# A hybrid decoder step on one core: another port rule in the planner, other feed-forward groups, squares summed by matmul, another attention order

## The chip, the cores and the metric

One core of a Trainium2 chip runs the whole program. The metric is the device time in microseconds of one execution. Of the kernel before there are three runs, and their median is the number that the change is measured against.

## What is computed

The reference is one inference step of a two-layer decoder trunk in fp32, for a prompt of 512 tokens and 8 samples of 8 new tokens each, at a width of 1024.

```python
def rms_norm(x, g):
    y = xf * lax.rsqrt(jnp.mean(xf * xf, axis=-1, keepdims=True) + EPS)
...
def swiglu(h, w_in, w_out):
    gate, up = jnp.split(h @ w_in, 2, axis=-1)
    return (jax.nn.silu(gate) * up) @ w_out
...
    for l in range(DEPTH):
        sh1, sc1, g1, sh2, sc2, g2 = ada_mod(c, ada_w[l], ada_b[l], 6)
        h = modulate(rms_norm(x, norm_g[l, 0]), sh1, sc1)
        if l < N_A_LAYERS:
            out, nbuf, h_last = recurrent_block(h, ...)
        else:
            q = apply_partial_rope((h @ attn_w_q[j]).reshape(B, T, N_HEADS, HEAD_DIM), pos)
            out = sliding_sink_attention(q, k_all, v_all, attn_sinks[j], p0) @ attn_w_o[j]
        x = x + g1[:, None, :] * out
        h = modulate(rms_norm(x, norm_g[l, 1]), sh2, sc2)
        x = x + g2[:, None, :] * swiglu(h, ffn_w_in[l], ffn_w_out[l])
```

After layer 0 a projection of the normalised stream gives keys and values, which layer 1 attends to over a window of 128. The feed-forward width is 2816, which is 22 chunks of 128.

## The kernel before, in words

The tokens are cut into two halves, h = 0 and h = 1 (A and B in the attention order), each of 256 prompt tokens and 32 sample tokens, 288 columns. The stream x lies transposed: 8 chunks of 128 features by 288 tokens for each half. Every large product is made of a rounded high part and a rest of each operand (`split`), and takes three matmuls for each chunk of 128 rows. So weights are first cast on ScalarE (ACT) into a high part and subtracted on VectorE (DVE) into a low part (`convert`, `operand`), and PE runs some 8000 matmuls of 288 columns.

The stages follow each other: start and adaLN products; the recurrent block in the order of the string `RNN` (x: conv inputs, g: the gates of a chunk, y: the gelu branch); its output product with residual; feed-forward layer 0; keys and values; queries and attention in the order of the string `ATT`; attention's output product; feed-forward layer 1; the last norm.

No engine call is issued where it stands. `Engine.record` (from L385) stores each with an estimated cost, and all appear in the profile under its line, L442. `Recorder.schedule` (from L213) then plans all of them as a list scheduler: at each step it takes for each engine, among the ready operations (up to 24 looked at), one with an early start and a low number, and emits the operations in the order of the planned starts. The plan knows the buffers, the delays between engines, and a port that DVE and GpSimd (POOL) share: an operation with `op.port` set starts no earlier than 130 ns before the port's last holder ends (L300) and then holds it (L331). `port` is set at L400 for POOL operations that read SBUF and for DVE operations with two wide SBUF inputs; an input that is also the output isn't counted. A changed cost or rule therefore moves instructions on all engines, in the whole program.

The places that the change touches besides:
- `square` (L778) squares a chunk of x on ACT after its residual and adds it on DVE to acc; `stats` (L789) sums over the features with three fp32 matmuls of acc with a vector of ones (one column out, for 128, 128 and 32 tokens), and `spread` takes the power on POOL, transposes it over the partitions on PE and copies it by ACT. `stats` is called for both halves after the recurrent block's output, after feed-forward 0 (`after_ffn0`, for keys and values) and after attention's output: six calls.
- `gates` (L1065) casts a chunk of the conv output into ta (ACT), subtracts into tb (POOL), and PE multiplies both with the gate weights; activations and a scan on DVE follow. Before it `evac_xr` does the conv: three SCALAR_TENSOR_TENSOR steps on DVE, in place, and small copies of carried columns on POOL.
- `ffn` (L1164) makes 22 chunks of the inner layer, and after each group of them (`GROUPS`, 6, 6, 6 and 4 chunks) the eight output units of that group for both halves (`out`): a unit is 3 matmuls for each chunk of the group, then a residual step. In the last group half 0 runs ahead by `LEAD` = 4 units.

## Time and profile before

| | us |
|---|---|
| median of 3 runs | 1288.2 (1283.86 to 1288.42) |
| the profiled execution: its time | 1286.79 |
| its span | 1285.0 |
| PE busy | 1247.7 (97%) |
| DVE busy | 891.7 (69%) |
| ACT busy | 655.9 (51%) |
| POOL busy | 485.7 (38%) |

The profiled execution's own time is 1.8 us above its span (what lies around the span) and 1.4 us under the median. Its mean granted TensorE clock is 0.987 of full speed. Of the chain of work that ended last, PE is 80% of the span, DVE 8% and ACT 5%. A busy share is a mean over stages, so the windows and timelines of the rows further below matter more than it.

### The profile page before, as it was taken

To read this page: it belongs to the slowest core of one execution; us is meant where nothing else is said; L and a number is where in the kernel's file an instruction comes from. 1 tells how busy PE (TensorE), PEld (TensorE's weight loads), DVE (VectorE), ACT (ScalarE), POOL (GpSimd) and SP (SyncE) were. 2 spreads that over 40 slices of the span, in tenths; PEclk is the share of its full clock that TensorE was granted. 3 is DMA by queue.
4 is the path that set the end of the run, shared out by engine and by line. 5 is a ranking of instruction groups with operands and counts; after the bars stand their busy time and mean duration, and the time that the engine had idled before them with its cause. 6 is when DMAs were issued, how large, how long until landed. Compare 5 with 4: busy or idle time off the path is not lost.

```text
span 1285.0 us, 25432 instructions
## 1 busy us (share of the span) xinstructions
PE 1247.7 (97%) x9532; PEld 1176.5 (92%) x9532; DVE 891.7 (69%) x2161; ACT 655.9 (51%) x1468; POOL 485.7 (38%) x710
## 2 busy tenths in 40 slices
PE   7898999999999999999999999999999999999997
PEld 5697889999999999999999988799999999999997
DVE  6886886687557546745769878657965765775767
ACT  4776884575234424522548668637642542552433
POOL 3455551114245135414424535200334633642422
PEclk9998999999999999999999999999999999999998
DMA  9944536335545755554441330323142332233222
GB/s 306 333 149 148 188 109 212 113 106 163 182 132 143 221 162 180 160 169 158 123 115 35 71 92 14 105 83 124 55 130 63 99 115 73 77 108 91 72 94 74
DMA packets 223981, 165.40 MB, mean 129 GB/s; under 512 B 23757, under 2 KB 209065, under 8 KB 223826
## 3 DMA queue, kind: packets, MB, share of 16 engines
q1 hardware_dynamic: 223410, 163.45, 42.1%
q8 instruction: 75, 1.23, 0.4%
q0 software_dynamic: 448, 0.32, 0.1%
q14 instruction: 48, 0.39, 0.1%
HBM read 160.85 MB, written 4.87 MB: 129 GB/s over the span
## 4 chain that ended last, share of the span: by engine, by line
PE 80%; DVE 8%; ACT 5%; POOL 2%; DMA 2%; issue 2%; SPq 1%; ACTq 0%; DVEq 0%; POOLq 0%
PE mm L442 76%; PE ada L442 4%; DVE sl L442 2%; DVE wh L442 2%; DVE ta L442 1%; POOL sl L442 1%; DMA raw<-in_ffn_w_in_dram 1%; DVE tb L442 1%; ACT tb L442 1%; ACT sl L442 1%; ACT wh L442 1%; ACT h L442 1%; SPq L442 1%; DMA reg<-in_x_prompt_dram 1%; ACT L442 1%
## 5 line engine op out<-in xcount | busy, mean ns | idle before, releaser
L442 PE MATMUL mm<-h,wh 128*128 128x288 f32 x4128 | 598.7, 300 | 9.7 <-DVE wh L442 5.6
L442 PEld LDWEIGHTS mm<-h,wh 128*128 128x128 f32 x4128 | 566.0, 190 | 27.8 <-issue 11.3
L442 PE MATMUL mm<-sl,wh 128*128 128x288 f32 x3218 | 459.5, 296 | 0.9 <-DVE sl L442 0.9
L442 PEld LDWEIGHTS mm<-sl,wh 128*128 128x128 f32 x3218 | 436.3, 188 | 7.5 <-issue 5.9
L442 ACT CAST wh<-raw 128x512 fp32r<-128x512 f32 (+2 forms) x388 | 268.0, 710 | 308.3 <-PE mm L442 210.2
L442 DVE TENSOR_TENSOR wh<-raw,wh 128x512 fp32r<-128x512 f32 (+2 forms) x388 | 346.4, 914 | 54.7 <-ACT wh L442 50.1
L442 DVE SCALAR_TENSOR_TENSOR x<-mm,mods,x 128x256 f32<-128x256 f32 x160 | 77.2, 482 | 149.9 <-PE mm L442 149.7
L442 POOL TENSOR_TENSOR raw<-raw 128x512 f32<-128x512 f32 x76 | 110.0, 1449 | 183.8 <-DVE wh L442 183.2
L442 POOL TENSOR_TENSOR x<-x,ta 128x32 f32<-128x32 f32 x152 | 53.5, 352 | 305.6 <-DVE ta L442 305.5
L442 POOL TENSOR_TENSOR raw<-raw,raw 128x512 f32<-128x512 f32 x76 | 112.3, 1477 | 3.8
L442 PE MATMUL mm<-tb,wh 128*128 128x288 f32 (+1 forms) x488 | 89.9, 299 | 5.9 <-POOL tb L442 5.0
L442 PEld LDWEIGHTS mm<-tb,wh 128*128 128x128 f32 x488 | 73.4, 190 | 7.7 <-POOL tb L442 5.5
L442 POOL TENSOR_TENSOR td<-td,td 128x288 f32<-128x288 f32 x38 | 31.9, 840 | 109.0 <-ACT td L442 109.0
L442 PE MATMUL mm<-ta,wh 128*128 128x288 f32 (+1 forms) x254 | 57.2, 302 | 0.0
L442 ACT ACTIVATE ta<-x 128x288 f32<-128x288 f32 x56 | 24.7, 444 | 56.4 <-POOL x L442 53.3
L442 DVE TENSOR_TENSOR td<-mm,td 128x288 f32<-128x288 f32 x76 | 33.8, 454 | 28.0 <-PE mm L442 27.8
L442 PE MATMUL ada<-reg,cz 128*32 128x512 f32 (+1 forms) x448 | 50.3, 553 | 0.2
L442 PEld LDWEIGHTS mm<-ta,wh 128*128 128x128 f32 x254 | 42.5, 191 | 3.4 <-ACT ta L442 1.7
L442 ACT COPY td<-mm 128x256 f32<-128x256 f32 (+1 forms) x102 | 33.2, 351 | 21.7 <-PE mm L442 18.7
L442 ACT ACTIVATE ta<-ta,stat 128x256 f32<-128x256 f32 (+2 forms) x72 | 32.3, 470 | 21.4 <-DVE stat L442 21.1
L442 DVE TENSOR_TENSOR sl<-td,sl 128x288 fp32r<-128x288 f32 x50 | 39.1, 782 | 6.0 <-ACT sl L442 5.4
L442 DVE TENSOR_TENSOR ta<-ta,mm 128x288 f32<-128x288 f32 x38 | 17.2, 453 | 28.8 <-PE mm L442 28.8
(202 smaller groups left out, 1249.1 us busy)
## 6 DMA issues: line engine op xcount, KB each, us to landing
raw<-in_ffn_w_in_dram SPq DMA_DIRECT2D x88, 512.0 KB
reg<-in_ada_w_dram SPq DMA_DIRECT2D x80, 512.0 KB
raw<-in_ffn_w_out_dram SPq DMA_DIRECT2D x48, 384.0 KB
raw<-in_rnn_w_in_dram SPq DMA_DIRECT2D x16, 512.0 KB
reg<-in_kv_ada_w_dram SPq DMA_DIRECT2D x16, 512.0 KB
wh<-in_ada_w_dram SPq DMA_DIRECT2D x24, 256.0 KB
raw<-in_rnn_w_out_dram SPq DMA_DIRECT2D x8, 512.0 KB
raw<-in_ffn_w_out_dram SPq DMA_DIRECT2D x16, 256.0 KB
```

The costliest lines, as they stand in the source:

```text
L442: self.rec.add(eng, lambda: getattr(obj, name)(*map(real, args), **{k: real(v) for k, v in kw.items()}), cost, outs, ins, func, lat, port, ...
```

## The change

Four parts. (1) In the planner, an operation's `port` is 0, 1 or 2. In-place inputs count now, so the conv steps on DVE are port operations. A DVE operation may start 130 ns before the port comes free, a POOL operation only 20 ns after it. POOL operations of up to 40 elements (`port` 2) don't hold the port; if it is held, their planned cost grows by the wait. (2) The square of the last chunk stays in a buffer of its own (`sq7`) instead of being added to acc, and `stats` has three more matmuls with ones for it. (3) The feed-forward groups are 5, 5, 6 and 6 chunks. (4) Another order of the jobs in attention.

```diff
--- before.py
+++ after.py
@@ -50,8 +50,8 @@
 WIN = 600
 
 RNN = "x0 x1 x2 g0 g1 x3 y0 y1 x4 g2 g3 x5 y2 x6 y3 g4 g5 x7 y4 y5 g6 g7 y7 y6"
-ATT = ("q0A q1A a0A q0B q2A a1A q1B a0B q3A a2A q2B a1B q4A a3A q3B a2B q5A a4A q4B a3B q6A a5A q5B a4B q7A a6A s0A q6B a5B s1A "
-       "a7A s2A q7B s3A s0B a6B fA s1B o0A s2B a7B s3B o1A fB o2A")
+ATT = ("q0A q2A a0A q1A q0B a2A a1A q1B q3A a0B q2B a1B q4A a3A a4A q3B a2B q5A q4B a3B q6A a5A q5B q7A a6A a4B s0A "
+       "q6B a5B s1A s2A s3A q7B a7A s0B a6B fA s2B a7B s1B o0A s3B o1A fB o2A")
 LOOK = {"PE": 24, "DVE": 24, "ACT": 24, "POOL": 24, "SP": 24}
 NRAW = 4
 NSL, NTA, NTB, NTD = 37, 7, 8, 4
@@ -230,6 +230,7 @@
         nxt = {k: 0 for k in self.kinds}
         got = set()
         cold = 0.0
+
 
         port, mode = 0.0, 0
         pos = {n: j for k in self.order for j, n in enumerate(self.order[k])}
@@ -297,8 +298,8 @@
                             break
                         continue
                     s = max(f, op.ready, at)
-                    if op.port:
-                        s = max(s, port - 130)
+                    if op.port == 1:
+                        s = max(s, port - 130 if e == "DVE" else port + 20)
                     if e == "PE" and op.mode != mode:
                         s = max(s, f + 100)
                     sw = e == "ACT" and op.func and op.func not in FREE_FUNCS and (table[0] is None or op.func not in TABLES[table[0]][1])
@@ -328,8 +329,10 @@
                 got.add(n)
             op.start = s
             cost = op.cost
-            if op.port:
+            if op.port == 1:
                 port = s + cost
+            elif op.port == 2 and s + 60 < port:
+                cost += port - s
             if e == "PE":
                 mode = op.mode
             if e == "PE":
@@ -396,8 +399,10 @@
         ps_ = any(_is_psum(x) for x in ins)
         func, lat = None, 0
 
-        wide = [x for x in ins if not _is_psum(x) and not str(x.space).endswith("DRAM") and (_free(x) > 1 or f == 1)]
+        reads = [x for x in (list(args) if "out" in kw else list(args[1:])) + [v for n, v in kw.items() if n not in ("out", "accum_out")] if isap(x)]
+        wide = [x for x in reads if not _is_psum(x) and not str(x.space).endswith("DRAM") and (_free(x) > 1 or f == 1)]
         port = eng == "POOL" and name != "dma_start" and bool(wide) or eng == "DVE" and not ps_ and (len(wide) > 1 or name == "tensor_scalar" and f > 1)
+        port = (2 if eng == "POOL" and f <= 40 else 1) if port else 0
         mode = 0
         if name == "matmul":
             if kw.get("start") is not True:
@@ -774,22 +779,30 @@
         return t.rearrange("p (b t) -> p b t", b=4)
 
 
+    sq7 = [None, None]
+
     def square(h, c):
         if c == 0:
             S.activation(acc[h][:], x[h][:, c, :], AF.Square)
         else:
             s = ta()
             S.activation(s.f[:, 0:HC], x[h][:, c, :], AF.Square)
-            V.tensor_tensor(acc[h][:], acc[h][:], s.f[:, 0:HC], ALU.add)
-            s.done()
+            if c == KC - 1:
+                sq7[h] = s
+            else:
+                V.tensor_tensor(acc[h][:], acc[h][:], s.f[:, 0:HC], ALU.add)
+                s.done()
 
     TOK = [slice(0, P), slice(P, 2 * P), slice(2 * P, HC)]
 
     def stats(h):
+        st = tst[h][:, 0:3]
         pt = aux()
-        st = tst[h][:, 0:3]
-        for t, ts in enumerate(TOK):
-            T.matmul(pt[0 : ts.stop - ts.start, t : t + 1], acc[h][:, ts], ones, start=True, stop=True)
+
+        for i, y in enumerate((acc[h], sq7[h].f)):
+            for t, ts in enumerate(TOK):
+                T.matmul(pt[0 : ts.stop - ts.start, t : t + 1], y[:, ts], ones, start=i + t == 0, stop=i == 1, skip_group_check=True)
+        sq7[h].done()
         V.tensor_scalar(st[:, 0:2], pt[:, 0:2], 1.0 / D, EPS, ALU.mult, ALU.add)
         V.tensor_scalar(st[0:32, 2:3], pt[0:32, 2:3], 1.0 / D, EPS, ALU.mult, ALU.add)
         spread(h)
@@ -1159,7 +1172,7 @@
 
 
 
-    GROUPS, PLAIN = (6, 6, 6, 4), 3
+    GROUPS, PLAIN = (5, 5, 6, 6), 3
 
     def ffn(l, g, after):
         wi, wo = a["ffn_w_in"][l], a["ffn_w_out"][l]
```

What this moves, at three places (the helper that records every operation is L442 before and L447 after). First the recurrent block's first gates, on PE. mm29 and mm30 are the two gate products of chunk 0, mm31 and mm32 those of chunk 1; ta is the cast and tb the rest of the conv output; mm34 and mm35 are other large products. Before:

```order
L442 MATMUL mm29_942<-ta29_926,wh19_718 128x300
L442 MATMUL mm29_942<-ta29_926,wh20_836 128x300
L442 MATMUL mm30_947<-ta29_926,wh21_771 128x300
L442 MATMUL mm30_947<-ta29_926,wh22_864 128x300
L442 MATMUL mm29_942<-tb25_934,wh19_718 128x300
L442 MATMUL mm30_947<-tb25_934,wh21_771 128x300
L442 MATMUL mm31_958<-ta31_932,wh19_718 128x300
L442 MATMUL mm31_958<-ta31_932,wh20_836 128x300
L442 MATMUL mm32_965<-ta31_932,wh21_771 128x300
L442 MATMUL mm32_965<-ta31_932,wh22_864 128x300
```

Now the first rows, and the rows around the tb products:

```order
L447 MATMUL mm29_931<-ta29_914,wh19_719 128x300
L447 MATMUL mm29_931<-ta29_914,wh20_819 128x300
L447 MATMUL mm30_939<-ta29_914,wh21_775 128x300
L447 MATMUL mm30_939<-ta29_914,wh22_857 128x300
L447 MATMUL mm34_944<-h01_323,wh23_918 128x288 x2
L447 MATMUL mm31_952<-ta31_937,wh19_719 128x300
L447 MATMUL mm31_952<-ta31_937,wh20_819 128x300
...
L447 MATMUL mm35_843<-h11_441,wh14_616 128x288
L447 MATMUL mm35_843<-h11_441,wh13_603 128x288 x2
L447 MATMUL mm29_931<-tb25_1020,wh19_719 128x300
L447 MATMUL mm30_939<-tb25_1020,wh21_775 128x300
L447 MATMUL mm35_843<-h11_441,wh14_616 128x288
```

The tb products stood right behind the ta products; now 39 large products of mm34 and mm35 and the ta products of chunk 1 stand between (the rows left out are of the same kinds). On POOL, 18 small operations of the conv stand between the last subtraction of h and the one into tb25, 13 before; on DVE the low part wh24 stands behind ten of the conv's steps, before behind twelve.

Second, DVE at the weight whose low part is wh36 (mm56 in the row of the high part wh35 on PE). ta and sl are gate operands of chunks, td11 a conv input. Before:

```order
L442 SCALAR_TENSOR_TENSOR sl25_1234<-sl26_1469,hA_81,ta38_1220 128x300
L442 TENSOR_TENSOR ta43_1403<-ta43_1403,sl34_1482 128x300
L442 SCALAR_TENSOR_TENSOR sl31_1352<-sl32_1479,ta41_1347 128x300
L442 TENSOR_TENSOR ta44_1452<-ta44_1452,sl25_1234 128x256
L442 SCALAR_TENSOR_TENSOR sl33_1415<-sl34_1482,ta43_1403 128x300
L442 TENSOR_TENSOR ta44_1452<-ta44_1452,sl25_1234 128x32
L442 SCALAR_TENSOR_TENSOR sl38_1574<-td11_1165,vecT_74,sl38_1574 128x300 x2
L442 TENSOR_TENSOR sl36_1643<-ta44_1452,sl35_1627 128x288
L442 SCALAR_TENSOR_TENSOR sl38_1574<-td11_1165,vecT_74,sl38_1574 128x300
L442 TENSOR_TENSOR wh36_1650<-raw18_1112,wh35_1559 128x1024
```

Now:

```order
L447 SCALAR_TENSOR_TENSOR sl37_1493<-td10_1110,vecT_74,sl37_1493 128x300
L447 SCALAR_TENSOR_TENSOR sl17_1031<-tb36_1517,sl17_1031 128x300
L447 SCALAR_TENSOR_TENSOR sl37_1493<-td10_1110,vecT_74,sl37_1493 128x300 x2
L447 TENSOR_TENSOR wh36_1556<-raw18_1127,wh35_1539 128x1024
L447 SCALAR_TENSOR_TENSOR tb36_1517<-sl33_1522,sl34_1530 128x300
L447 SCALAR_TENSOR_TENSOR sl38_1558<-td11_1158,vecT_74,sl38_1558 128x300
L447 SCALAR_TENSOR_TENSOR ta38_1260<-ta38_1260,sl16_965 128x300
L447 SCALAR_TENSOR_TENSOR ta41_1328<-ta41_1328,sl10_898 128x300
L447 TENSOR_TENSOR ta38_1260<-ta38_1260,sl26_1397 128x300
L447 TENSOR_TENSOR ta41_1328<-ta41_1328,sl32_1405 128x300
```

The steps of ta38, ta41 and ta43 with their SCALAR_TENSOR_TENSOR rows (scans among them) stood ahead of wh36; now they come behind it.

Third, PE at the end of feed-forward 0, from half 0's sums of squares (mm249) to the first key/value product (h03); mm250 holds the transposes of `spread`, mm251 to mm255 are the last output units. Before:

```order
L442 MATMUL mm253_8317<-sl201_8045,wh269_8174 128x288
L442 MATMUL mm249_8342<-small_67,acc0_69 128x1 x2
L442 MATMUL mm249_8342<-small_67,acc0_69 32x1
L442 MATMUL mm254_8350<-sl189_7633,wh270_8191 128x288
L442 MATMUL mm254_8350<-sl190_7649,wh270_8191 128x288
...
L442 MATMUL mm254_8350<-sl202_8053,wh270_8191 128x288
L442 MATMUL mm250_8370<-ident_66,tst0_71 128x128 x2
L442 MATMUL mm250_8370<-ident_66,tst0_71 128x32
L442 MATMUL mm254_8350<-sl201_8045,wh271_8200 128x288
...
L442 MATMUL mm255_8379<-sl202_8053,wh272_8252 128x288
L442 MATMUL mm255_8379<-sl201_8045,wh273_8265 128x288
L442 MATMUL mm258_8436<-h03_8412,wh274_8282 128x288
L442 MATMUL mm259_8438<-h03_8412,wh278_8346 128x288
```

Now:

```order
L447 MATMUL mm248_8234<-sl203_7954,wh273_8232 128x288
L447 MATMUL mm249_8264<-small_67,acc0_69 128x1 x2
L447 MATMUL mm249_8264<-small_67,acc0_69 32x1
L447 MATMUL mm251_8212<-sl198_7861,wh264_7898 128x288
...
L447 MATMUL mm252_8279<-sl185_7384,wh266_7930 128x288
L447 MATMUL mm249_8264<-small_67,ta245_8277 128x1 x2
L447 MATMUL mm249_8264<-small_67,ta245_8277 32x1
L447 MATMUL mm252_8279<-sl186_7405,wh266_7930 128x288
...
L447 MATMUL mm253_8317<-sl181_7249,wh269_8119 128x288
L447 MATMUL mm250_8323<-ident_66,tst0_71 128x128 x2
L447 MATMUL mm250_8323<-ident_66,tst0_71 128x32
L447 MATMUL mm253_8317<-sl185_7384,wh268_8106 128x288
```

Before, 11 large products stood between the sums and the transposes, and 13 between the transposes and the first product of h03. Now 9 stand between acc's sums and those of the last square (ta245), 17 from there to the transposes, and 51 from the transposes to the first product of h03.

## Rows read from the trace of the kernel before

**Rows 1.** The page, busy us, share of the span and instructions of each engine.

```profile
PE 1247.7 (97%) x9532; PEld 1176.5 (92%) x9532; DVE 891.7 (69%) x2161; ACT 655.9 (51%) x1468; POOL 485.7 (38%) x710
```

**Rows 2.** Windows: span, busy us (instructions) per engine, granted clock, DMA share, GB/s.

```profile
660.00:680.00 20.00, 16.54 (x113) 15.53 (x112) 15.44 (x44) 13.17 (x28) 7.48 (x14) 0.95 0.46 116
680.00:700.00 20.00, 20.00 (x149) 19.74 (x149) 17.53 (x49) 14.75 (x40) 7.59 (x9) 0.97 0.19 41
780.00:800.00 20.00, 19.41 (x174) 16.86 (x174) 15.03 (x65) 17.75 (x65) 12.57 (x25) 1.00 0.08 22
800.00:820.00 20.00, 17.81 (x134) 13.72 (x130) 13.48 (x63) 13.98 (x54) 8.40 (x24) 0.91 0.36 103
1000.00:1020.00 20.00, 20.00 (x152) 20.00 (x152) 15.61 (x24) 11.41 (x25) 13.65 (x10) 1.00 0.32 90
```

**Rows 3.** The same table for the recurrent block, and the sum over it.

```profile
60.00:80.00 20.00, 19.17 (x127) 17.97 (x127) 12.84 (x22) 14.35 (x29) 11.08 (x26) 0.83 0.50 157
...
100.00:120.00 20.00, 15.97 (x112) 13.01 (x105) 14.76 (x27) 12.34 (x26) 14.23 (x32) 0.87 0.67 217
120.00:140.00 20.00, 19.90 (x147) 18.22 (x146) 14.57 (x31) 15.17 (x28) 9.42 (x22) 0.96 0.31 97
...
160.00:180.00 20.00, 18.01 (x134) 16.16 (x133) 15.98 (x27) 15.74 (x30) 11.93 (x25) 0.99 0.25 79
180.00:200.00 20.00, 19.84 (x140) 19.61 (x139) 18.43 (x40) 15.92 (x26) 8.29 (x23) 0.93 0.74 227
sum 140.00, PE 131.39 PEld 120.40 DVE 109.96 ACT 105.79 POOL 75.41; mean PE 18.77 PEld 17.20 DVE 15.71 ACT 15.11 POOL 10.77
```

**Rows 4.** Timeline of PE, 52 to 62: start, length, instruction, [idle time before, releaser].

```profile
60.83 0.87 PE L442 MATMUL mm<-tb,wh 128*128 128x300 f32 x2 [2.99 <-POOL tb L442]
```

**Rows 5.** Timeline of DVE, 52 to 62.

```profile
53.58 5.38 DVE L442 SCALAR_TENSOR_TENSOR sl<-td,vecT,sl 128x300 f32<-128x300 f32 x12
```

**Rows 6.** Timeline of POOL, 52 to 62.

```profile
54.10 0.49 POOL L442 COPY xtail<-td 128x3 f32<-128x3 f32 x1
...
58.54 3.01 POOL L442 TENSOR_TENSOR tb<-sl,ta 128x300 fp32r<-128x300 f32 x2
61.50 0.18 POOL L442 COPY pco<-td 128x3 f32<-128x3 f32 x1
```

**Rows 7.** Timeline of PE, 108 to 118.

```profile
116.54 1.81 PE L442 MATMUL mm<-h,wh 128*128 128x288 f32 x6 [4.03 <-DVE wh L442]
```

**Rows 8.** Timeline of DVE, 108 to 118.

```profile
115.28 1.21 DVE L442 TENSOR_TENSOR wh<-raw,wh 128x1024 fp32r<-128x1024 f32 x1
```

**Rows 9.** Timeline of POOL, 108 to 118.

```profile
112.93 2.10 POOL L442 TENSOR_TENSOR tb<-sl,ta 128x300 fp32r<-128x300 f32 x2
```

**Rows 10.** Timeline of PE, 170 to 180.

```profile
179.36 0.52 PE L442 MATMUL mm<-tb,wh 128*128 128x300 f32 x1 [1.99 <-POOL tb L442]
```

**Rows 11.** Timeline of POOL, 170 to 180.

```profile
175.64 1.85 POOL L442 COPY ho<-sl 128x1 f32<-128x1 f32 x4
```

**Rows 12.** Timeline of PE, 664 to 682.

```profile
668.89 0.73 PE L442 MATMUL mm<-small,acc 128*128 128x1 f32 x6
669.54 1.71 PE L442 MATMUL mm<-sl,wh 128*128 128x288 f32 x11
671.90 0.60 PE L442 MATMUL mm<-ident,tst 128*128 128x128 f32 x3 [0.65 <-POOL tst L442]
...
677.19 4.98 PE L442 MATMUL mm<-h,wh 128*128 128x288 f32 x24 [2.77 <-ACT h L442]
```

**Rows 13.** Timeline of POOL, 664 to 682.

```profile
669.95 1.90 POOL L442 TENSOR_TENSOR tst<-tst,small 128x3 f32<-128x3 f32 x1 [1.52 <-DVE tst L442]
```

**Rows 14.** Timeline of PE, 1270 to 1286.

```profile
1275.33 1.01 PE L442 MATMUL mm<-ident,x 128*128 128x128 f32 x6 [0.54 <-DVE ta L442]
1276.70 0.76 PE L442 MATMUL mm<-small,acc 128*128 128x1 f32 x6 [0.36 <-DVE acc L442]
```

**Rows 15.** Timeline of PE, 798 to 818.

```profile
806.19 0.32 PE L442 MATMUL mm<-ta,reg 128*64 128x160 f32 x1 [2.12 <-ACT sl L442]
```

## The prediction

> **What bounds the kernel now.** I read the busy row of the page first. TensorE (PE) is busy 97% of the span, VectorE (DVE) 69% [rows 1]. So time can come from three places: instructions that PE no longer executes, stretches in which PE stands idle, and stretches in which it runs at the lower of its two clock levels (1.2 instead of 2.4 GHz). Then I read the table of 20 us windows. Its first number after the length is PE's busy time, and the granted clock stands before the DMA share. In the feed-forward part a window is full (20.00 us, 152 rows, so a product every 0.132 us) at clock 1.00 [rows 2]: nothing is to be had there. The lost time lies in the recurrent block (60 to 200 us) [rows 3], at the hand-over to the key/value part (660 to 700) and at the end of attention (800 to 820) [rows 2], each with idle time and a clock under 1. Last I read the timelines of PE at these places, where the bracket gives the idle time and its releaser, and the timelines of the engine named.
>
> Four stalls carry the argument.
> - S1: PE idles 2.99 us before the product with the gate remainder tb, which comes from POOL [rows 4]. POOL was late because its small copies took 0.49 us each while DVE ran twelve three-operand conv steps back to back [rows 5, 6]; the same copy takes 0.18 us when DVE is at something else [rows 6].
> - S2: PE idles 4.03 us for a weight's low part from DVE [rows 7]. That subtraction takes 1.21 us and began only at 115.28 [rows 8], behind steps of DVE that alternated with two POOL subtractions (2.10 us for two) [rows 9].
> - S3: 1.99 us, again for tb from POOL [rows 10], which stood behind four copies that took 1.85 us [rows 11].
> - S4: after the sums of squares PE idles 0.65 us for POOL's power and then 2.77 us for the first normalised chunk [rows 12]; the power itself takes 1.90 us [rows 13].
>
> The lower clock adds to this. A window of 20 us at clock c loses 20(1-c): 3.4 us in 60:80; 2.6 + 0.8 in 100:120 and 120:140; 0.2 + 1.4 in 160:180 and 180:200 [rows 3]; 1.0 + 0.6 in 660:680 and 680:700; 1.8 in 800:820 [rows 2]. Of the first two a part (0.4 and 1.0 us by my estimate) fell into the idle time itself. So S1 is worth 6.0 us, S2 6.4, S3 3.6, S4 5.0; S1 to S3 together 16.0.
>
> **The change, part by part.** All times stand against the profiled execution, 1286.8 us; the median of the runs is 1288.2, 1.4 us above, and I move the sum over unchanged.
>
> *Scheduler's port rule, S1.* PE's last product before the wait ended at 60.83 - 2.99 = 57.84 [rows 4]. Now 39 other products and the four of the next chunk's first half stand between the gate's first half and its tb products, so PE comes to them at 57.84 + 43 x 0.132 = 63.5. POOL has five more small instructions ahead of tb: its start moves from 58.54 to 61.1 at most (5 x 0.52), and with 1.5 us for one of the two [rows 6] tb is there by 62.6. The inserted products need weight wh24, whose low part moved up on DVE from behind the twelfth conv step to behind the tenth: ten steps of 0.45 us from 53.6 [rows 5] and 1.2 us for the part end near 59.3, and PE, with 16 products from 57.3 on, arrives there near 59.4. I take all of S1: -6.0 (bounds 0, if the wait reappears at the next tb, and -6.0).
>
> *S2.* The weight's low part (wh36) now stands ahead of the chain of steps it was behind, and products stand ahead of the adaLN group. But everything that was ahead of it is still to be done by the same two engines: busy time in 60:200 is 110 us on DVE and 75 on POOL of 140 (the sum in [rows 3]). I take half: -3.2 (bounds 0 and -6.4).
>
> *S3 and what the gates get in exchange.* Its tb comes 60 products earlier than its use, but three other tb's in the middle of the stage are now issued late and their products deferred. S3 going (-3.6) against a new wait of the size of S3: 0 (bounds -3.6 and +3.6). For the deferred gates, whose scans end 26 products (26 x 0.132 = 3.4 us) later at the end of the stage, I add +1.5 (bounds 0 and +3.4). Recurrent block: -6.0 - 3.2 + 0 + 1.5 = -7.7.
>
> *Groups of 5, 5, 6, 6: S4.* The number of products does not change; the number of output units and evacuations does not either, and their loads carry the same bytes in other pieces (of 64 KB for each chunk of a unit). What changes is that a unit of the last group has 18 products instead of 12, so that the lead of four units is 72 products instead of 48. In the new order the chain from the last sum to the transposes has 17 products beside it (2.2 us; it took 669.54 to 671.90, 2.36 us [rows 12]), and the one from there to the first key/value product has 51 (6.7 us, against 677.19 - 671.90 = 5.3 us). Both idle times and the lower clock after them go: -5.0 (bounds -3 if the transposes still wait, and -5.0). The second half's sums come with products behind them; no stall. Inside the two feed-forward layers: 0, since PE is full there [rows 2]; bounds -1 and +2 for loads that come later or earlier.
>
> *The tail.* At the end DVE falls behind units of 12 products (1.6 us each); PE idles 0.54 and 0.36 us for it [rows 14]. With 18 products (2.4 us) DVE keeps up: -0.9 (bounds 0 and -0.9).
>
> *Squares.* Six calls of the sums get three more products with ones each; DVE loses six adds, of which none is named as a releaser of PE in the rows. Three such products moved the next one from 668.89 to 669.54, 0.65 us [rows 12]. PE is full where they stand, so they cost 6 x 0.65 = +3.9 (bounds 0, if they only fill idle time, and +4.4). The Trainium skill ("TensorE: Matmul & The Clock Gate", section "Back-to-back issue gap") gives a product of 1 to 64 columns some 60 cycles, 25 ns; two instructions for each product make 0.15 us a call and +0.9 us in all, and by that the sum below would be 3.0 us lower. The row contradicts it here, so the row counts. The new products wait for ACT's square of the last chunk; they are queued 9 products behind the first three at S4, so nothing waits behind them there.
>
> *Attention's order.* Before, the run of small transposes and score products with no large product beside it is, counted in the order of PE's instructions, 87 long at the end, and PE idles 2.12 us in it [rows 15] and loses 1.8 us by the clock [rows 2]. Now the longest runs are 70 at the end and 42 earlier. A run of 34 lies in 780:800, where PE lost 0.6 us [rows 2]. The end may gain up to 4, the new run may lose as much: 0 (bounds -4 and +4).
>
> **Sum:** -7.7 - 5.0 - 0.9 + 3.9 + 0 + 0 = -9.7, so 1277.1 for the profiled execution and **1278.5 us** for the median.
>
> **The rivals.** (a) *The shared port is full.* POOL's copies and DVE's two-input steps slow each other [rows 6, 9], so in the recurrent block an order cannot help if together they need the whole stage; the stalls only move. Their busy times, 185 us in 140, speak for it, but contain time that one engine spent blocked by the other. Then the -7.7 is 0, and the sum is -2.0: 1286.2. The Trainium skill ("SBUF — State Buffer", section "Who interferes with whom") says that a two-input DVE instruction and a GpSimd instruction that reads SBUF exclude each other, the second one blocked wholly; the 0.49 against 0.18 us agree with the direction. (b) *All three stalls go and no new one comes:* -16.0 instead of -7.7, sum -18.0: 1270.2. The copies' 0.18 us alone speaks for it, the loaded DVE against it. (c) *Slower: PE runs out in the recurrent block.* The gates' remainders come later in the new order (the first after 41 more products, the scans 26 later), and when PE has used up its independent products there, it waits and then runs at the lower clock. S2 gives the price of one such wait, 6.4 us. It decides against the change when these waits grow by more than 8.4 us over the old 16.0 (a slowdown of 6.4 and the 2.0 gained elsewhere); with two more, 12.8 - 2.0 = +10.8: 1299.0. Against it: the cover at S1 is counted in the new order. (d) *The change does not do what it says,* in that the stall at S4 persists because DVE, not the number of products, is late there: -9.7 + 5.0 = -4.7: 1283.5.
>
> **How the numbers follow.** Chances: my forecast 0.42, (a) 0.22, (b) 0.14, (c) 0.11, (d) 0.11. About 0.5% (6.4 us) is what a measurement of this kernel can tell from no change: faster means under 1281.8, slower over 1294.6. Faster: 0.42 x 0.9, all of (b), and a quarter of (a) and (d): 0.60. Slower: (c) less a little, 0.10. The rest, 0.30, is the same. The likeliest case's own range, from its bounds, is 1272 to 1284. To hold 8 in 10 the range takes in (b) with 3 us of attention's bound, 1267, and (a) with its +4 and 0.7 to spare, 1291; (c) is what is left out.
>
> **What would show it.** Right: no idle time of PE above 1 us before a tb product near 60 us, clock 1.0 in 60:80 and in 660:700, first key/value product within 0.3 us of the one before it, sums of squares as two groups of about 0.65 us. Wrong: idle times that sum to 9 us or more in 60:200, as now, or one over 3 us with a clock under 0.9 behind it; over 4 us of idle time in attention's run of 42; PE idle at 300 to 660 for a weight.

## The result, and the profile after

The change took the median from 1288.2 to 1278.23 us (five runs each, 1275.33 to 1280.35 against 1283.86 to 1288.6): a ratio of 0.9927, 95% interval 0.9908 to 0.9946. The forecast was 1278.5. The profiled execution took 1275.33 us with a span of 1273.5, which is 11.5 us less span than before. The page's span and busy row, which answer to [rows 1]:

```profile
span 1273.5 us, 25461 instructions
...
PE 1246.1 (98%) x9568; PEld 1172.8 (92%) x9568; DVE 905.7 (71%) x2156; ACT 659.4 (52%) x1469; POOL 488.2 (38%) x709
```

PE is busy 1.6 us less in all, although 36 instructions were added, so 9.9 of the 11.5 us are time in which it had waited. Where, is shown by the windows that answer to [rows 3] and [rows 2] (busy time of each engine, granted clock, DMA share, GB/s). First the recurrent block:

```profile
60.00:80.00 20.00, 20.00 (x151) 18.37 (x152) 14.76 (x28) 17.22 (x34) 15.44 (x30) 1.00 0.72 223
...
100.00:120.00 20.00, 20.00 (x151) 18.08 (x150) 18.19 (x38) 18.05 (x36) 14.04 (x33) 1.00 0.60 204
120.00:140.00 20.00, 20.00 (x152) 18.39 (x151) 17.61 (x35) 18.90 (x35) 11.15 (x26) 1.00 0.57 191
140.00:160.00 20.00, 17.91 (x135) 14.38 (x134) 14.80 (x29) 15.79 (x29) 12.44 (x28) 1.00 0.46 153
160.00:180.00 20.00, 19.19 (x144) 18.94 (x144) 16.07 (x33) 17.72 (x32) 7.40 (x18) 1.00 0.54 177
180.00:200.00 20.00, 20.00 (x153) 18.20 (x152) 15.64 (x34) 10.51 (x19) 5.74 (x19) 1.00 0.39 117
sum 140.00, PE 137.10 PEld 124.72 DVE 115.08 ACT 113.86 POOL 80.64; mean PE 19.59 PEld 17.82 DVE 16.44 ACT 16.27 POOL 11.52
```

PE is full up to 140 us and at clock 1.00 in the whole block: S1, S2 and S3 are gone, and with them every stretch of the block at the lower level. A new wait stands in 140:160 (17.91 us busy, 19.48 in before). Then the hand-over, attention's end and two windows of feed-forward 1:

```profile
660.00:680.00 20.00, 18.43 (x125) 17.30 (x124) 17.80 (x48) 14.77 (x35) 8.83 (x11) 0.91 0.25 54
680.00:700.00 20.00, 18.32 (x139) 17.82 (x138) 17.50 (x46) 16.95 (x45) 9.59 (x10) 1.00 0.26 57
800.00:820.00 20.00, 19.75 (x167) 17.88 (x165) 10.88 (x44) 10.40 (x36) 3.41 (x10) 1.00 0.31 87
860.00:880.00 20.00, 19.15 (x144) 18.53 (x143) 14.42 (x38) 15.59 (x40) 2.43 (x3) 1.00 0.39 140
900.00:920.00 20.00, 19.20 (x143) 18.73 (x142) 17.26 (x20) 10.31 (x21) 12.20 (x9) 1.00 0.29 84
```

The hand-over is not repaired (18.43 and 18.32 us, clock 0.91), attention's end is full, and feed-forward 1 now has holes, where every window was full before.

How much each stretch is worth can be read by counting products. Both programs have 8088 matmuls of 288 or 300 columns. Below is the start of the nth of them in the profiled run of each kernel, minus the start of the nth one in before (us; counted in the trace's PE timeline; the order of single products differs, so tenths mean little; each line is one execution, which lies up to 3 us from the median of its kernel). The nth product of before starts at 206.8 (1000th, end of the recurrent block), 296.3 (1600th), 646.7 (4000th, ahead of the hand-over), 709.7 (4400th), 856.3 (5000th, after attention) and 1259.5 us (8000th).

| kernel | 1000 | 1600 | 4000 | 4400 | 5000 | 8000 | last |
|---|---|---|---|---|---|---|---|
| the change | -13.5 | -12.1 | -12.3 | -10.6 | -18.0 | -9.6 | -10.1 |
| port rule alone | -13.6 | -13.5 | -10.6 | -9.1 | -5.0 | +0.4 | +0.3 |
| groups alone | -2.4 | -2.4 | -4.1 | -8.6 | -9.0 | -8.0 | -8.4 |
| squares alone | +1.2 | +2.5 | +2.2 | +2.2 | +9.0 | +12.2 | +12.2 |
| attention's order alone | -1.3 | -1.3 | -1.2 | -0.6 | -7.2 | -6.8 | -6.9 |
| new rule only till feed-forward 0, groups, order | -13.1 | -13.1 | -14.4 | -18.9 | -25.1 | -23.9 | -24.3 |
| the change without squares | -12.6 | -12.6 | -11.3 | -9.0 | -11.3 | -6.1 | -6.5 |
| a cost + 1 ns | +0.7 | +0.7 | +1.3 | +1.3 | +1.1 | +1.2 | +1.2 |
| a cost - 1 ns | -3.8 | -3.8 | -3.5 | -3.6 | -3.6 | -3.6 | -3.6 |
| new rule only from feed-forward 0 on | -0.6 | -0.6 | +2.6 | +4.1 | +7.8 | +13.4 | +13.3 |
| rank half of the rule alone | -3.2 | -3.4 | +0.4 | +6.5 | +10.8 | +16.5 | +16.5 |
| in-place half of the rule alone | -14.8 | -14.7 | -14.9 | -14.5 | -13.6 | -13.5 | -13.5 |
| the sums' matmuls twice | -0.2 | +0.8 | +1.0 | +0.9 | +0.9 | +2.0 | +2.1 |

The first line is the result by stage: -13.5 in the recurrent block, +1.2 in feed-forward 0, +1.7 at the hand-over, -7.4 in attention, +8.3 in feed-forward 1, -0.5 to the last product, and -1.4 from there to the end of the span (10.5 us before, 9.1 after). The clock moves such a line too, beside the plan: at the 120th product (54.8 us) the change is 1.9 us behind; its granted clock was 0.50 in 20:30, where before had 0.88.

### The profile page after: what moved, and what is told of

It is laid out like the page before. It is cut to its first block, busy times and chain, and to the rows that moved or that the text cites. A ratio compares the mean times of both kernels' runs of the same rounds, so it can differ in the third digit from the quotient of the medians.

```text
span 1273.5 us, 25461 instructions
## 1 busy us (share of the span) xinstructions
PE 1246.1 (98%) x9568; PEld 1172.8 (92%) x9568; DVE 905.7 (71%) x2156; ACT 659.4 (52%) x1469; POOL 488.2 (38%) x709
## 4 chain that ended last, share of the span: by engine, by line
PE 73%; DVE 13%; ACT 6%; POOL 4%; issue 2%; DMA 1%; SPq 0%; ACTq 0%; POOLq 0%; DVEq 0%
PE mm L447 69%; PE ada L447 4%; DVE wh L447 4%; DVE sl L447 4%; POOL raw L447 3%; ACT wh L447 2%; DVE ta L447 1%; DMA reg<-in_x_prompt_dram 1%; DVE td L447 1%; ACT tb L447 1%; ACT h L447 1%; ACT sl L447 1%; ACT ta L447 1%; DVE tb L447 1%; DVE h L447 1%
## 5 line engine op out<-in xcount | busy, mean ns | idle before, releaser
L447 PE MATMUL mm<-h,wh 128*128 128x288 f32 x4128 | 596.8, 299 | 3.5 <-ACT h L447 2.1
L447 PEld LDWEIGHTS mm<-h,wh 128*128 128x128 f32 x4128 | 562.4, 189 | 21.7 <-issue 9.9
L447 PE MATMUL mm<-sl,wh 128*128 128x288 f32 x3218 | 462.4, 296 | 0.8 <-ACT ta L447 0.8
L447 PEld LDWEIGHTS mm<-sl,wh 128*128 128x128 f32 x3218 | 436.9, 188 | 9.4 <-issue 5.9
L447 ACT CAST wh<-raw 128x512 fp32r<-128x512 f32 (+3 forms) x388 | 266.4, 710 | 292.4 <-PE mm L447 208.4
L447 DVE TENSOR_TENSOR wh<-raw,wh 128x512 fp32r<-128x512 f32 (+3 forms) x388 | 344.9, 913 | 60.1 <-ACT wh L447 54.0
L447 POOL TENSOR_TENSOR raw<-raw 128x512 f32<-128x512 f32 x76 | 109.8, 1445 | 183.9 <-DVE wh L447 154.1
L447 POOL TENSOR_TENSOR x<-x,ta 128x32 f32<-128x32 f32 x152 | 58.7, 386 | 306.8 <-DVE ta L447 306.7
L447 DVE SCALAR_TENSOR_TENSOR x<-mm,mods,x 128x256 f32<-128x256 f32 x160 | 77.3, 483 | 133.2 <-PE mm L447 132.1
L447 POOL TENSOR_TENSOR raw<-raw,raw 128x512 f32<-128x512 f32 x76 | 111.8, 1471 | 3.7
L447 PE MATMUL mm<-tb,wh 128*128 128x288 f32 (+1 forms) x488 | 89.7, 299 | 4.5 <-POOL sl L447 1.6
L447 PEld LDWEIGHTS mm<-tb,wh 128*128 128x128 f32 x488 | 72.3, 188 | 9.4 <-DVE td L447 5.4
L447 POOL TENSOR_TENSOR td<-td,td 128x288 f32<-128x288 f32 x38 | 32.0, 843 | 111.9 <-ACT td L447 106.5
L447 ACT ACTIVATE ta<-x 128x288 f32<-128x288 f32 x56 | 24.3, 443 | 67.2 <-POOL x L447 62.1
L447 PE MATMUL mm<-ta,wh 128*128 128x288 f32 (+1 forms) x254 | 55.9, 298 | 0.0
L447 DVE TENSOR_TENSOR td<-mm,td 128x288 f32<-128x288 f32 x76 | 33.2, 452 | 27.9 <-PE mm L447 27.9
L447 PE MATMUL ada<-reg,cz 128*32 128x512 f32 (+1 forms) x448 | 49.5, 553 | 0.0
L447 DVE TENSOR_TENSOR sl<-ta,sl 128x288 fp32r<-128x288 f32 x54 | 44.9, 834 | 1.7 <-ACT sl L447 1.5
L447 ACT COPY td<-mm 128x256 f32<-128x256 f32 (+1 forms) x102 | 34.2, 353 | 20.4 <-PE mm L447 18.4
L447 DVE TENSOR_TENSOR sl<-td,sl 128x288 fp32r<-128x288 f32 x50 | 38.2, 764 | 8.1 <-ACT sl L447 8.1
L447 ACT ACTIVATE ta<-mm 128x288 f32<-128x288 f32 x54 | 21.4, 410 | 43.2 <-PE mm L447 41.8
L447 PEld LDWEIGHTS mm<-ta,wh 128*128 128x128 f32 x254 | 41.5, 188 | 1.8 <-ACT wh L447 0.8
```

What stands on the lines that cost most here:

```text
L447: self.rec.add(eng, lambda: getattr(obj, name)(*map(real, args), **{k: real(v) for k, v in kw.items()}), cost, outs, ins, func, lat, port, ...
```

## The experiments

**The four parts, each alone on the kernel before.** The port rule (part 1):

```diff
-                    if op.port:
-                        s = max(s, port - 130)
+                    if op.port == 1:
+                        s = max(s, port - 130 if e == "DVE" else port + 20)
...
+            elif op.port == 2 and s + 60 < port:
+                cost += port - s
...
+        reads = [x for x in (list(args) if "out" in kw else list(args[1:])) + ...]
...
+        port = (2 if eng == "POOL" and f <= 40 else 1) if port else 0
```

> Kernel before with the planner's port rule alone (part 1 of the change). Theory A, each part acts at the place it names: the recurrent block's stalls go, PE is 11 to 14 us ahead of before at its 1000th product (13.5 with the whole change), and nothing else moves by more than 2 us; so 1274 to 1278. Rival B, any new deal of the plan moves stalls all over the program: the curve against before goes up and down by 3 us or more in attention and feed-forward too, and the sum is anything between 1275 and 1292.

Measured: 1286.98 against 1288.18 us, ratio 0.9992 (0.9979 to 1.0004). The recurrent part of theory A holds (-13.6 at the 1000th product), the rest doesn't: all of it is given back, 3 us in feed-forward 0, 1.5 at the hand-over, 4 in attention and 5.3 in feed-forward 1, as rival B describes. Alone the rule is worth nothing.

Groups:

```diff
-    GROUPS, PLAIN = (6, 6, 6, 4), 3
+    GROUPS, PLAIN = (5, 5, 6, 6), 3
```

> Kernel before with feed-forward groups 5, 5, 6, 6 alone. Theory A: nothing until the end of feed-forward 0; the hand-over to keys and values gains what the prediction gave it or, if DVE and ACT are late there as the trace of the whole change suggests, about 2 us; the tail 0.9; so 1283 to 1288. Rival B: the units of the first groups and their earlier demand move the plan in the recurrent block too, by 3 us or more either way.

Measured: 1279.5 us, ratio 0.9931 (0.9912 to 0.9951), faster than theory A's range. 4.5 us of the 8.4 come between the 4000th and the 4400th product; PE's timeline there (start, length, instruction, idle time before and its releaser in brackets), to be held against [rows 12]:

```profile
660.97 0.70 PE L442 MATMUL mm<-small,acc 128*128 128x1 f32 x6
661.60 1.59 PE L442 MATMUL mm<-sl,wh 128*128 128x288 f32 x10
663.03 0.55 PE L442 MATMUL mm<-ident,tst 128*128 128x128 f32 x3
663.51 5.56 PE L442 MATMUL mm<-sl,wh 128*128 128x288 f32 x40
668.91 3.22 PE L442 MATMUL mm<-h,wh 128*128 128x288 f32 x20
```

No bracket is left: 40 products lie between the transposes and the first key/value product where 13 had been. Another 2.4 us come in the recurrent block, which the groups don't touch, and 1.7 in feed-forward 0. The 2.4 us are the clock's and not the groups': S1, S2 and S3 stand there as before (2.99, 4.02 and 1.99 us), but the products behind them lost less by the clock. The 70 behind S1, at 0.91 granted in 60:80 where before had 0.83, first in this run, then in before:

```profile
62.96 9.91 PE L442 MATMUL mm<-h,wh 128*128 128x288 f32 x70
```

```profile
62.99 11.20 PE L442 MATMUL mm<-h,wh 128*128 128x288 f32 x70
```

Squares:

```diff
+            if c == KC - 1:
+                sq7[h] = s
...
+        for i, y in enumerate((acc[h], sq7[h].f)):
+            for t, ts in enumerate(TOK):
+                T.matmul(..., y[:, ts], ones, start=i + t == 0, stop=i == 1, skip_group_check=True)
```

> Kernel before with the last chunk's squares kept apart and summed in the product with ones, alone. Theory A: six calls of 0.65 us more on PE, +3.9, and where the second group waits for ACT's square up to 1 us more for each such call: 1291 to 1294. Rival C, the new products fill time in which PE waits anyway, and DVE's six adds less shorten the chain: 1286 to 1289.

Measured: 1298.22 us, ratio 1.0071 (1.0052 to 1.009), above both. 2.7 us come at the two pairs of calls in full stretches (1.3 between the 1000th and the 1600th product, 1.4 behind the 5000th); but 6.8 come between the 4400th and the 5000th, in attention, where there is no call. No matmul was added there, so what is left is a new deal of the plan; which instruction of it costs the time was not followed. Another 1.8 us come later in feed-forward 1.

Attention's order:

```diff
-ATT = ("q0A q1A a0A q0B q2A a1A q1B a0B q3A a2A ...
+ATT = ("q0A q2A a0A q1A q0B a2A a1A q1B q3A a0B ...
```

> Kernel before with the attention order alone. Theory A: the whole gain of attention that the whole change shows (7.4 us between the 4400th and the 5000th product) comes from the order: 1280 to 1283. Rival D, it comes from the port rule, which takes the POOL steps of the softmax out of DVE's way: 1286 to 1289 here.

Measured: 1281.34 us, ratio 0.9943 (0.9925 to 0.9961): theory A. 6.6 us come between the 4400th and the 5000th product. The window that answers to the one of 800:820 in [rows 2], with the sum of the five windows of 720 to 820, in the run with the order alone:

```profile
800.00:820.00 20.00, 19.78 (x153) 16.73 (x154) 13.31 (x72) 15.65 (x61) 5.87 (x19) 0.91 0.45 127
sum 100.00, PE 99.27 PEld 87.49 DVE 81.98 ACT 75.68 POOL 45.14; mean PE 19.85 PEld 17.50 DVE 16.40 ACT 15.14 POOL 9.03
```

The same sum of the kernel before:

```profile
sum 100.00, PE 95.78 PEld 81.90 DVE 77.83 ACT 72.36 POOL 43.38; mean PE 19.16 PEld 16.38 DVE 15.57 ACT 14.47 POOL 8.68
```

PE's idle time in these 100 us falls from 4.2 to 0.7 us. That this comes near the change's 7.4 us doesn't make the order their only cause: the port rule alone loses 4.1 us in attention, and in the change the squares give some 5 back (below).

**Does the rest come from the plan's sensitivity?** One planned cost changed by 1 ns, up and down:

```diff
-            cost = (52 if ps_ else 94) + 0.8333 * f + ...
+            cost = (53 if ps_ else 94) + 0.8333 * f + ...
```

> Kernel before with one number of the planner's costs changed by 1 ns (an ACT operation that reads PSUM is planned at 53 instead of 52 ns plus its length). Nothing in the program but the order can change. Theory A: within 2 us of before. Rival B (the plan is so sensitive that any change of it deals the stalls anew): 4 us or more either way, with jumps at attention and in the recurrent block.

> The same with 51 ns. Theory A: within 2 us of before. Rival B: 4 us or more either way, and not the mirror image of the run with 53.

Measured: 1288.31 (ratio 1.0012, 0.9997 to 1.0027) and 1284.6 us (0.998, 0.9965 to 0.9996) against 1287.16. The run with 51 lies between the two theories. So a meaningless change of the plan moves the time by up to 3 us, and nearly all of it ahead of the 200th product (73.5 us). The place is S1: with 51 ns its wait of 2.99 us shrinks to two short ones, and the clock is 1.00 in 60:80.

```profile
57.23 0.82 PE L442 MATMUL mm<-ta,wh 128*128 128x300 f32 x4 [0.33 <-ACT ta L442]
58.61 0.54 PE L442 MATMUL mm<-tb,wh 128*128 128x300 f32 x2 [0.55 <-POOL tb L442]
```

So S1 can go by an accident of the plan, without any new port rule; S2 (4.03 us) and S3 (1.98 us) stay in that run. Neither run moved attention or feed-forward 1 by more than 0.2 us. Two draws don't bound what a larger new deal may do there.

**The change without the squares.** The squares' part of the diff taken back.

> The whole change without the squares. Theory A (the squares cost six times 0.65 us on PE and up to 2 us of waits for ACT's square): 1272 to 1275 against 1278.2. Rival E (the squares cost 10 us as they do alone): 1266 to 1270. Rival B (a new deal): outside both, above 1277.

Measured: 1276.87 us against 1287.16, ratio 0.9926 (0.9903 to 0.9948); the change had 0.9927 (0.9908 to 0.9946). The ranges of A and E are missed, that of B too by a hair. The squares' own price is saved (the curve doesn't rise between the 1000th and the 1600th product), but attention gains 2.3 us instead of 7.4. By the ratios the squares cost the change nothing that can be told; the profiled execution of this run was the slowest of the four, 1278.85 us.

**Where the port rule gains and where it loses.** The rule was limited by a flag that the recorder sets when feed-forward 0's pairs begin; operations recorded under the old rule keep the old one (`port` 3). First with the new rule ahead of that point only, with the new groups and order and without the squares:

```diff
+        self.old = False
...
+                    elif op.port == 3:
+                        s = max(s, port - 130)
...
+        if self.rec.old:
+            wide = [x for x in ins if ...]
+            port = 3 if ... else 0
...
         def emit():
+            rec.old = True
```

> New groups and new attention order, no squares in the product; the new port rule only for operations recorded before feed-forward 0's pairs, the old rule after that. Theory A (the port rule gains 13.5 us in the recurrent block and loses about as much behind it by the plans that it makes there, groups gain 7, attention's order 6, all of it at their own places): the gains add up, -13.5 - 7 - 6, so 1260 to 1264. Rival B (each new deal of the plan scatters stalls anew): 1268 to 1280.

Measured: 1261.09 us against 1287.16, ratio 0.9803 (0.9788 to 0.9818): theory A, and the fastest kernel of the study. Its windows:

```profile
60.00:200.00 140.00, 137.10 (x1024) 124.67 (x1023) 115.46 (x226) 113.89 (x211) 80.74 (x181) 1.00 0.55 177
...
640.00:720.00 80.00, 79.72 (x620) 75.89 (x620) 68.78 (x227) 59.09 (x152) 34.98 (x56) 1.00 0.31 70
```

The hand-over, 3.7 us short of full in 640:720 before, lacks 0.3. With the rule everywhere the parts do not add up like this: at the last product the rule, the groups and the order alone sum to -15.0 us, and the three together (the change without squares) have -6.5; some 5 us of the difference lie in the recurrent block, 2.4 of them the clock's, and some 5 at the hand-over.

Then the reverse, the kernel before with the new rule from that point on:

> Kernel before with the new port rule only from feed-forward 0's pairs on, the old rule ahead of it (the reverse of the split in the 1261 us version). Theory A (the rule's plan puts DVE's two-input steps under POOL's long subtractions from there on): no gain up to the 1600th product, then 9 to 14 us lost in the hand-over, attention and feed-forward 1, so 1296 to 1302, with the splits sl from ta at 1.1 us each in feed-forward 1 as in the run with the rule alone. Rival B (those losses came from the state in which the recurrent block's new plan ended): within 4 us of before.

Measured: 1299.95 against 1287.87 us, ratio 1.0094 (1.0058 to 1.0131): theory A, with losses at the same places as in the run with the rule alone. The step that shows it is DVE's split of gate times up into a high and a low part, sl from ta, whose durations in feed-forward 1 (840 to 1240; count, ns minimum/median/maximum, first and last start, shapes) are in before:

```profile
L442 DVE TENSOR_TENSOR sl<-ta,sl x18: 446/449/683, 935.8 to 1235.2; 128x288 fp32r<-128x288 f32 x18
```

and in the run with the rule from feed-forward 0 on:

```profile
L453 DVE TENSOR_TENSOR sl<-ta,sl x17: 451/1542/1554, 947.2 to 1237.1; 128x288 fp32r<-128x288 f32 x17
```

The same instruction takes 1.54 instead of 0.45 us. The expectation had named 1.1 us, the mean of the run with the rule alone; there are two kinds, 6 of the 17 near 0.45 us and 11 near 1.54, so the mean describes neither.

**Which half of the rule.** The first half without counting in-place inputs:

```diff
+        port = (2 if eng == "POOL" and f <= 40 else 1) if port else 0
```

(with the schedule lines of part 1, and `wide` left as before)

> One half of the port rule alone: DVE may start 130 ns before the port comes free, POOL only 20 ns after; POOL's small operations neither hold it nor are let in free; in-place inputs still not counted. Theory F (the recurrent gain comes from POOL's small copies no longer being planned as holders): 8 us or more ahead of before at the 1000th product. Theory G (it comes from counting the conv's in-place steps): 3 us or less there.

Then the second half by itself:

```diff
-        wide = [x for x in ins if not _is_psum(x) ...]
+        reads = [x for x in (list(args) if "out" in kw else list(args[1:])) + ...]
+        wide = [x for x in reads if not _is_psum(x) ...]
```

> The other half alone: in-place inputs counted, the old 130 ns for both engines and no class 2. Theory F: 5 us or less ahead of before at the 1000th product, or behind it, since the copies now also queue for the conv's steps in the plan. Theory G: 8 us or more ahead.

Measured: the rank half 1303.46 us, ratio 1.0119 (1.0093 to 1.0145); the in-place half 1276.04 us, ratio 0.9902 (0.9874 to 0.993), both against 1287.87. Theory G: counting the conv's in-place steps is enough for the recurrent block's gain (-14.8) and loses nearly nothing behind it (+1.3). That execution was 2.7 us faster than the median of its kernel, and by the medians the in-place half gains 11.8 us in all. The rank half gains 3.2, no more than the run with 51 ns, and loses 19.7; it holds two things, the unequal bounds of DVE and POOL and the small operations that don't hold the port, and which of them loses was not tried. The in-place half doesn't make the conflicts fewer: POOL's copies of 128x3 take a median of 0.46 us between 45 and 200 us with it and in before. What it changes is the order. The split in feed-forward 1, first with the rank half, then with the in-place half:

```profile
L446 DVE TENSOR_TENSOR sl<-ta,sl x16: 451/1540/1555, 950.1 to 1229.8; 128x288 fp32r<-128x288 f32 x16
```

```profile
L443 DVE TENSOR_TENSOR sl<-ta,sl x19: 444/450/680, 922.3 to 1231.2; 128x288 fp32r<-128x288 f32 x19
```

**The price of the sums.** Each of the 18 matmuls issued twice in its place, nothing else moved:

```diff
             T.matmul(pt[0 : ts.stop - ts.start, t : t + 1], acc[h][:, ts], ones, start=True, stop=True)
+            rec.ops[-1].emit = lambda e=rec.ops[-1].emit: (e(), e())
```

> Kernel before with the same plan; only each of the 18 matmuls of the six sums with ones is issued twice in its place, the second overwriting the first with the same value. So 18 matmuls more on PE, as the squares add, and no instruction moved. Theory A: 0.65 us for a call of three, +3.9 at the last product, 1291 to 1293. By the page's 25 ns an instruction: +0.9. Either way the other 8 us that the squares cost alone are the new deal.

Measured: 1289.98 against 1287.87 us, ratio 1.0017 (1.0 to 1.0034); 2.3 us between the 1000th and the last product, between the two values. PE's timeline at the first call, and at the hand-over:

```profile
234.59 1.22 PE L442 MATMUL mm<-small,acc 128*128 128x1 f32 x12
235.74 1.60 PE L442 MATMUL mm<-sl,wh 128*128 128x288 f32 x10
```

```profile
669.88 1.24 PE L442 MATMUL mm<-small,acc 128*128 128x1 f32 x12
671.04 1.73 PE L442 MATMUL mm<-sl,wh 128*128 128x288 f32 x11
673.40 0.60 PE L442 MATMUL mm<-ident,tst 128*128 128x128 f32 x3 [0.62 <-POOL tst L442]
...
678.68 3.60 PE L442 MATMUL mm<-h,wh 128*128 128x288 f32 x23 [2.77 <-ACT h L442]
```

Twelve instructions hold the next product up for 1.15 us where six did for 0.64 (235.44 - 234.80 in before): 0.5 us for the second six, which stand right behind the first. At the hand-over the two brackets, 0.62 and 2.77 us, are as long as in [rows 12]; the curve doesn't move there (+1.0 to +0.9).

## Why the prediction was right, and where its steps were not

The sum was right, -9.7 forecast and -10.0 measured by the medians; several of its terms were not, and their errors cancel. That the sum came so close is luck: the recurrent block and attention gained 13 us more than forecast, the hand-over and feed-forward lost 12 us more (the squares counted there). By its own steps:

*S1, right.* PE's timeline of the change at the first gates:

```profile
58.89 0.82 PE L447 MATMUL mm<-ta,wh 128*128 128x300 f32 x4
...
60.48 5.12 PE L447 MATMUL mm<-h,wh 128*128 128x288 f32 x37
65.45 0.44 PE L447 MATMUL mm<-tb,wh 128*128 128x300 f32 x2
```

The products of mm34 and mm35 fill the time, and the tb products start at 65.45 without a bracket. From the 120th to the 160th product, which stand on either side of S1, the curve falls from +1.9 to -3.9 us: 5.8 us, where S1 was put at 6.0. The run with 51 ns gets 4.4 us of this at the same place. One term was rough: "1.5 us for one of the two" is a mean, and in the trace the first of the two tb steps took 2.23 us and the second 0.82; by the prediction's own working tb was then due at 63.3, just ahead of PE at 63.5. S2 is gone too: the window 100:120 is full.

*The recurrent block, mis-sized.* "Half" of S2 and +1.5 for the deferred gates made -7.7; it was -13.5, near rival (b)'s -16.0. What fell short of (b) are the 1.9 us by which the change comes late to the block and the wait which the prediction set against S3:

```profile
156.32 0.54 PE L447 MATMUL mm<-tb,wh 128*128 128x300 f32 x2 [1.63 <-POOL sl L447]
...
159.18 0.55 PE L447 MATMUL mm<-tb,wh 128*128 128x300 f32 x2 [0.46 <-POOL tb L447]
...
167.77 2.66 PE L447 MATMUL mm<-sl,wh 128*128 128x288 f32 x18 [0.81 <-ACT ta L447]
```

1.63, 0.46 and 0.81 us, 2.9 in sum, but at full clock. Against them four short waits of before (0.18, 0.81, 0.52 and 0.88 us) are gone too, which the prediction left out: -16.0 + 1.9 + 2.9 - 2.4 = -13.6. The step that failed is rival (a)'s argument inside the forecast, that the same work on two engines cannot be dealt better: DVE and POOL are busy longer in 60:200 than before (115 and 81 us against 110 and 75) and PE still waits less, since what it waits for comes first. The in-place half alone is enough for this; the rank half is not. Nor do the rows show what (a) said of both engines: beside DVE's steps POOL's copies are slowed [rows 6], but the steps themselves follow each other every 0.45 us.

*S4, right alone and wrong in the change.* The cover of more products works: 4.5 us with the groups alone, -5.0 forecast. In the change the hand-over lost 1.7 us instead; PE's timeline there:

```profile
654.32 0.60 PE L447 MATMUL mm<-ident,tst 128*128 128x128 f32 x3
654.85 7.03 PE L447 MATMUL mm<-sl,wh 128*128 128x288 f32 x51
661.71 0.96 PE L447 MATMUL mm<-h,wh 128*128 128x288 f32 x6
663.48 0.53 PE L447 MATMUL mm<-h,wh 128*128 128x288 f32 x2 [0.81 <-ACT wh L447]
664.77 2.60 PE L447 MATMUL mm<-h,wh 128*128 128x288 f32 x8 [0.76 <-ACT h L447]
```

17 and 51 products stand there as counted and the first key/value product has no bracket. But six products later a weight from ACT is late, and then a chunk of h, and the clock falls (0.91 in 660:680). Rival (d) described this outcome, with DVE late; here the releaser is ACT. That the port rule is behind it is shown by the kernel with the old rule from feed-forward 0 on, whose hand-over is whole; the squares, which it lacks too, are not it, since the change without them lost 2.3 us there. The prediction had read the first product's cover and not how fast the chunks follow each other.

*Tail, right and a little small:* -0.9 forecast, -1.4 from the last product to the end of the span. In place of 0.54 and 0.36 us [rows 14] one wait is left:

```profile
1266.14 0.76 PE L447 MATMUL mm<-small,ta 128*128 128x1 f32 x6 [0.25 <-ACT ta L447]
```

*Squares, the price right, what else they do missed.* In the change the six new groups of matmuls hold the next instruction up by 0.63, 0.58, 0.58, 0.69, 0.60 and 0.69 us (start to start), 3.8 in sum; one of them:

```profile
651.10 0.65 PE L447 MATMUL mm<-small,ta 128*128 128x1 f32 x6
651.69 2.53 PE L447 MATMUL mm<-sl,wh 128*128 128x288 f32 x17
```

The repeated matmuls, each group right behind its like, came to 2.3 us, since they cost 0.5 a call and filled a wait at the hand-over. The 25 ns an instruction that the Trainium skill gives ("TensorE: Matmul & The Clock Gate", section "Back-to-back issue gap") would make it 0.9 and is too low here, as the row had said; the section itself gives it for an isolated product, without the load of the stationary operand. That nothing waits for the second group holds at the hand-over, for which the prediction said it; after attention's output, where it didn't look, PE waits for ACT's square:

```profile
866.10 0.65 PE L447 MATMUL mm<-small,acc 128*128 128x1 f32 x6
...
870.20 0.76 PE L447 MATMUL mm<-small,ta 128*128 128x1 f32 x6 [0.85 <-ACT ta L447]
```

*Attention, wrong.* Put at 0 with bounds of 4 us, it gained 7.4. Counting the longest run without a large product was a poor measure; the order alone takes away 3.5 us of idle time in 720 to 820 and 6.6 us by the products. In the change the port rule (+4.1 alone) and the squares (some -5) come on top of that and nearly cancel. What the new run of 42 cost by itself can't be told apart; PE lacks only 0.25 us in the window 800:820 of the change.

*Feed-forward, wrong.* "0, since PE is full there" was the largest error: +8.3 in feed-forward 1. About 5.5 of it is the rank half of the port rule, which costs this in every run that has it from there on (+5.3, +5.5 and +5.7 between the 5000th and the 8000th product, +5.2 in the change without squares) and little in those that lack it and the squares too (+0.1 to +1.2); 1.5 and the 0.85 us above belong to the squares. A full engine shows that there is nothing to gain; it doesn't show that a new plan loses nothing. The change's own rows, DVE and then POOL, in the middle of that layer:

```profile
1094.49 1.19 DVE L447 TENSOR_TENSOR sl<-td,sl 128x288 fp32r<-128x288 f32 x1
1095.60 1.54 DVE L447 TENSOR_TENSOR sl<-ta,sl 128x288 fp32r<-128x288 f32 x1
```

```profile
1093.57 3.27 POOL L447 TENSOR_TENSOR raw<-raw,raw 128x512 f32<-128x512 f32 x2
```

DVE's two splits (0.45 us each by themselves) stand under POOL's two subtractions and take 1.19 and 1.54 us. Where DVE is late, PE waits for its step td, which reads the sums that the next products of tb are added to:

```profile
912.83 1.06 PE L447 MATMUL mm<-tb,wh 128*128 128x288 f32 x6 [0.34 <-DVE td L447]
```

Most of these waits are too short for a bracket. Counted from start to start, 25 products of tb between the 5000th and the 8000th start 5.1 us later in all than the usual 0.133 us would have them, 2.0 us of it in brackets; the three runs above have 5.1, 4.9 and 4.9 us there, and before has none.

So rival (b) nearly holds for the recurrent block and (d) for the hand-over; (a) and (c) fell. What stays open is why the squares move attention by +6.8 us alone and by -5 with the rest: the 1 ns runs show no such jump, and it wasn't followed further. Nor were the two things in the rank half taken apart, nor was the in-place half with groups and order run without the limit, which the table suggests as the next kernel.

## What to carry to other kernels

When a planner deals all instructions anew, judge a change by stage and by part: 11.5 us of span less were 22.8 us of gains and 11.2 us of losses, and taking the new rule only where it gains gave 1261 us. Count an in-place operand as a read when modelling a shared port; and test a rule on a saturated stage too, where its only possible effect is a loss. Before a gain is put down to a rule, change the plan by something meaningless too: here 1 ns took most of S1 away. A curve of the nth product against the kernel before shows in one look which stage moved.

## What the runs showed of the hardware

Not expected was how much a port conflict costs the engine that comes second: one 128x288 subtraction on DVE took a median of 1.54 us under POOL's subtractions, 0.45 without, and each of the slow ones ended 0.31 to 0.32 us after the end of the POOL instruction that it stood under (11 of the 17 in the run with the rule from feed-forward 0 on). POOL's pair took 3.27 us in the change and 2.99 in before (at 1096.39), where one subtraction of DVE's stood beside it as well. The Trainium skill ("SBUF — State Buffer", section "Who interferes with whom") says that the one that comes second is blocked wholly; 1.54 - 0.45 = 1.09 us of waiting behind subtractions of some 1.5 us agrees. And six one-column fp32 matmul instructions behind six others cost 0.5 us, 0.08 us each; between large products, six cost 0.58 to 0.69 us. The same wait of 2.99 us was followed by 70 products in 11.20 us in one execution and in 9.91 us in another, at a granted clock of 0.83 and 0.91 in that window: what a wait costs by the clock is not the same each time.
